# A decoder trunk in split fp32: more weight pairs by seven products, sums by DMAs that add, and an order with later loads

## The chip, the cores and the metric

One core of one Trainium2 chip runs the whole kernel. The metric is the device time of one execution in microseconds (us). The kernel before took 2121.14 us, the median of 3 runs (2120.87 to 2121.73).

## The reference

Two layers act on a residual stream x of 256 tokens by 2048 columns, all in float32. Each layer has a token mixer and an MLP, each behind an RMS norm and added to x. The mixers (forgetting attention in layer 0, dilated windows in layer 1) are not touched by the change. The MLPs are:

```
def sq_relu_mlp(h, w_up, w_down):
    a = jax.nn.relu(h @ w_up)
    return (a * a) @ w_down

for i in range(DEPTH):                      # 2 layers
    h = rms_norm(x, mix_norm_g[i])
    ...                                     # mixer
    x = x + mix
    h = rms_norm(x, mlp_norm_g[i])
    x = x + sq_relu_mlp(h, mlp_w_up[i], mlp_w_down[i])
```

h is 256 x 2048, w_up 2048 x 8192, w_down 8192 x 2048.

## The kernel before

**Split numbers.** Each fp32 operand is a high part (rounded to fp32r, a format that TensorE, PE, multiplies fast) and a low part, the rest. A product is three matmuls: high by high, low weight by high, high weight by low token (L386 to L388). `loaded` (L329) brings a pair of weight blocks (2 x 128 rows by 512 columns, 512 KB) into a raw buffer by a DMA on SP's queue; `cut` (L340) has ScalarE (ACT) cast the high part `hi` (L342) and VectorE (DVE) subtract it for the low part `lo` (L348). There are 6 raw, 4 hi and 4 lo buffers, and one more of each in the MLPs.

**Units.** A `Unit` (L352) makes 256 tokens by 512 columns from 8 such pairs. In the form `whole` (L376) a pair is 12 matmuls of 512 columns. In the form `parts` (L410) the pair's 2 x 2 blocks (two row blocks by two column halves, against two token tiles) are multiplied by seven products and not eight, a Strassen-Winograd scheme: DVE first makes three sums of weight blocks (L413 of 512 columns, L418 and L420 of 256) in a second raw buffer, two cuts follow (768 columns of the weights themselves, 1024 of sums), and PE runs 21 matmuls of 256 columns. The token sums (`sigma`) are made once per MLP. A unit that mixes both forms (`quarters`, L391, for its full pairs) needs the banks A and C and some additions at its end (L973 to L986). `HALVED` (L42) names the pairs of each up unit that go by seven products: 5 of 8 in the periods 1 to 3 of each MLP, none in period 0, so 120 pairs in the two MLPs.

**An MLP** (L1016) has 4 periods; each makes 4 up units (2048 of 8192 columns), and the 4 down units of the period before are merged in, a unit of each at a time, pair by pair in the order `UU_D`. The last period's down units stand alone at the end. At an up unit's end (`up_end`, L944) ACT brings the sums from PSUM, applies ReLU, DVE transposes blocks of 32 (L994), DMAs take the tile through DRAM and back (`through_dram`, L444), ACT squares (L1002), casts the high part of the tokens aT (L1007), and DVE makes the low part (L1009). At a down unit's end (`add_to_x`, L521) DVE adds both PSUM banks to x (L527).

**The order** is worked out while the program is built. `Plan` (L89) holds every operation with a cost in us (`on_act`, `on_dve`, `moved`, `WHOLE`, `QUARTER`); PE's products keep the order in which the code adds them, and every other operation gets a due time backwards from the product that needs it (`gap`: HANDOFF between engines, LANDING after a DMA). A forward pass (`run`) then takes, on each engine, the ready operation that is due first, and its times give each engine's fixed list. Engines run their lists in order and wait for each other by semaphores.

Of the kernel before, what the change touches and what calls it, by code (L numbers as in the profile page):

```python
# [13 lines left out]
ALU = mybir.AluOpType  # L14
# [3 lines left out]
P = 128  # L18
D = 2048
S = 256  # L20
NT = S // P
NC = 512
# [13 lines left out]
PERIODS = DFF // D  # L36
WHOLE = 6 * 0.2167
QUARTER = 0.112
ADDING = ()
FIVE = (0, 2, 4, 5, 7)  # L40
MORE = (1, 1, 1)
HALVED = [[(), (), (), ()], [FIVE] * 4, [FIVE] * 4, [FIVE] * 4]  # L42


def on_act(n, accum=False):
    return 0.24 + 0.00083 * n + (0.19 if accum else 0)


def on_dve(n, inputs=2):
    return 0.17 + (0.00104 if inputs == 2 else 0.00054) * n  # L50


def moved(kb):
    return kb / 380.0

# [33 lines left out]
class Plan:  # L89

    HANDOFF = 0.25
    LANDING = 2.1
    BACKLOG = 2.0
    FIRST = 14.0

# [39 lines left out]
    def gap(self, a, b):  # L137
        if a.eng == "dma":
            return self.LANDING
        if a.eng is None:  # L140
            return 0.0
        if a.eng == b.eng:
            return 0.0 if a.eng == "pe" else 0.06
        return self.HANDOFF

# [37 lines left out]
    def run(self):  # L183
# [18 lines left out]
        while events:  # L202
# [14 lines left out]
            if eng == "dma":  # L217
                landed = max(landed, now) + op.us
                free[eng] = max(now + 0.07, landed - self.BACKLOG)
# [9 lines left out]
def trunk(ctx: ExitStack, tc, x, fox_w_in, fox_b_f, fox_q_gain, fox_k_gain, fox_w_out, dil_w_in,  # L229
# [30 lines left out]
    N_HI = 4  # L260
    N_LO = 4
    N_Z = 1
    N_C = 1
# [7 lines left out]
    for ph in ("mlp0", "mlp1"):  # L271
        rings[ph] = dict(sigma=ring("sigma", 4, 2 * 4 * 2 * P, ph), tr=ring("tr", 4, NT * NC, ph),
                         z=ring("z", N_Z, 6 * S, ph), c=ring("c", N_C, NC, ph))
    for ph, n_sets, heads in (("fox", 1, 4), ("dil", 3, 2)):
# [169 lines left out]
    def through_dram(turned, into, size=NT * NC):  # L444
        blocks = blocks_ring.take()
        for i in range(4):
            def go(i=i):
                nc.sync.dma_start(v(blocks)[:, :, :, i, :].rearrange("t j c x -> c t j x"),
                                  v(turned)[32 * i:32 * i + 32, 0:size].rearrange("p (t j x) -> p t j x", t=NT, j=4))
            add("dma", 0.45, go, reads=[turned], writes=[(blocks, i)])  # L450

# [68 lines left out]

    def add_to_x(n, then=None):  # L521
        def end(banks):
            pair = banks[0].slot[0]

            def go():
# [417 lines left out]

    def up_end(l, phase, source, halved):  # L944
        own = rings[phase]

        def end(banks):
            z, turned = own["z"].take(), own["tr"].take()
            by = lambda t: v(f"rstd{l}")[:, t:t + 1]
# [50 lines left out]
            for t in range(NT):  # L1000
# [7 lines left out]
                writes=[(a, b, 0) for b in range(4)])  # L1008
            add("dve", on_dve(2 * NC), lambda: nc.vector.tensor_sub(r(a)[:, 2 * NC:], v(turned), v(a)[:, 0:2 * NC]),  # L1009
                reads=[*((turned, t) for t in range(NT)), *((a, b, 0) for b in range(4))], writes=[(a, b, 1) for b in range(4)])  # L1010
        return end

    AC, BE = ("A0", "A1", "C0", "C1"), ("B0", "B1")
    UU_D = "UUDUDUDUDUDUDUDD"

    def mlp(l, layer, phase, source, sigmas, then, last=None):  # L1016
# [6 lines left out]
        for b in range(PERIODS):  # L1023
            a = Source()
            ups = []
            for n in range(4):
                halved = HALVED[b][n]
                banks = AC if halved else ("A0", "A1") if b or n % 2 == 0 else ("B0", "B1")
                ups.append(Unit(source, mlp_w_up[layer], 0, [(b * D + n * NC, NC)], banks,
                                up_end(l, phase, a, halved), halved, sigmas))  # L1030
            if b == 0:
# [8 lines left out]
            for n in range(NX):  # L1040
                banks = ("E0", "E1") if turn % 2 == 0 else ("B0", "B1")
                turn += 1
                end = add_to_x(n, then if b == PERIODS - 1 else None)
                downs.append(Unit(a, mlp_w_down[layer], b * D, [(n * NC, NC)], banks, end, adding=ADDING if b < PERIODS - 1 else ()))
# [216 lines left out]
```

## Time and profile before

| | |
|---|---|
| runs, median (lowest to highest) | 2121.14 us (2120.87 to 2121.73) |
| profiled execution, its own time | 2121.22 us |
| its span, first to last instruction | 2119.5 us |
| PE busy | 2109.8 us (100%) |
| DVE busy | 1669.8 us (79%) |
| ACT busy | 1266.0 us (60%) |
| POOL busy | 57.8 us (3%) |
| DMA packets of SP's queue | 72.9% of 16 engines, 490.86 MB |
| granted PE clock | 1.00 |

PE is TensorE, PEld its weight loads, POOL is GpSimd, SP the engine that issues the DMAs. Busy shares are means over stages: in the merged periods of the MLPs (464 to 947 us in the first) DVE is busier than its mean. In a view of groups each row has line, engine, operation, out<-in, shape and count, then busy us, mean ns of one, and idle us before them with what ended it. In a list of waits a row has who waited for whom, us in total, times, longest.

### The profile page before, as it was taken

Reading aid. Unit: us, or ns where it says so; the run is one execution under the profiler, and the core shown is the slowest. Engines: PE = TensorE matmul, PEld = TensorE weight load, DVE = VectorE, ACT = ScalarE, POOL = GpSimd, SP = SyncE. Lnnn points to the kernel's source line nnn. Section 1 sums busy time; section 2 is a strip of 40 time slices with the busy share of each in tenths; the row PEclk is TensorE's granted clock in tenths of the full one; section 3 lists DMA queues with packets and bytes.
Section 4 is the critical chain, followed back from the end, with each engine's and each line's share of the span. In section 5 each row is a group of like instructions: output and inputs, shape, how many; then the busy total and the mean of one; then the engine's idle time right before and its main releaser. Section 6 shows DMA issues by size and latency. Waiting matters only on the chain.

```text
span 2119.5 us, 30432 instructions
## 1 busy us (share of the span) xinstructions
PE 2109.8 (100%) x11285; PEld 1888.0 (89%) x11285; DVE 1669.8 (79%) x2092; ACT 1266.0 (60%) x1640; POOL 57.8 (3%) x51
## 2 busy tenths in 40 slices
PE   9999999999999999999999999999999999999999
PEld 7888888889999999998888888888899999999988
DVE  6777777678899899886787777777678898898874
ACT  5555556566666666666555555556666666666652
POOL 1011000000000000000010000000000000000000
PEclk9999999999999999999999999999999999999999
DMA  7777668777767777777786776768767777777773
GB/s 247 233 221 199 212 217 262 240 243 238 228 225 242 241 225 237 245 257 260 227 259 200 235 223 207 249 203 285 237 223 232 249 228 230 248 229 228 248 259 129
DMA packets 336133, 492.93 MB, mean 233 GB/s; under 512 B 21928, under 2 KB 137712, under 8 KB 335984
## 3 DMA queue, kind: packets, MB, share of 16 engines
q1 hardware_dynamic: 335712, 490.86, 72.9%
q8 instruction: 88, 1.44, 0.3%
q14 instruction: 61, 0.50, 0.1%
q10 hardware_dynamic: 272, 0.13, 0.0%
HBM read 455.26 MB, written 35.65 MB: 232 GB/s over the span
## 4 chain that ended last, share of the span: by engine, by line
PE 99%; DMA 0%; SPq 0%; DVE 0%; issue 0%; ACT 0%
PE bank_B L386 11%; PE bank_B L388 11%; PE bank_B L387 11%; PE bank_C L407 9%; PE bank_A L386 7%; PE bank_A L388 7%; PE bank_A L387 7%; PE bank_E L386 7%; PE bank_E L388 7%; PE bank_E L387 7%; PE bank_A L437 3%; PE bank_A L438 3%; PE bank_A L436 3%; PE bank_C L437 2%; PE bank_C L438 2%; PE bank_C L436 2%
## 5 line engine op out<-in xcount | busy, mean ns | idle before, releaser
L342 ACT CAST hi<-raw 128x1024 fp32r<-128x1024 f32 (+1 forms) x720 | 736.0, 1026 | 585.0 <-PE bank_B L388 171.1
L348 DVE TENSOR_TENSOR lo<-raw,hi 128x1024 fp32r<-128x1024 f32 (+1 forms) x720 | 854.7, 1193 | 277.1 <-ACT hi L342 261.7
L386 PE MATMUL bank_A<-hi,hT 128*128 128x512 f32 x552 | 212.0, 384 | 0.0
L388 PE MATMUL bank_A<-hi,hT 128*128 128x512 f32 x552 | 210.3, 381 | 0.0
L387 PE MATMUL bank_A<-lo,hT 128*128 128x512 f32 x552 | 210.2, 381 | 0.0
L386 PE MATMUL bank_B<-hi,aT 128*128 128x512 f32 x520 | 197.5, 380 | 0.5 <-ACT aT L646 0.5
L388 PE MATMUL bank_B<-hi,aT 128*128 128x512 f32 x520 | 197.1, 379 | 0.0
L387 PE MATMUL bank_B<-lo,aT 128*128 128x512 f32 x520 | 197.1, 379 | 0.0
L386 PE MATMUL bank_B<-hi,hT 128*128 128x512 f32 x480 | 183.7, 383 | 0.0
L387 PE MATMUL bank_B<-lo,hT 128*128 128x512 f32 x480 | 181.9, 379 | 0.0
L388 PE MATMUL bank_B<-hi,hT 128*128 128x512 f32 x480 | 181.9, 379 | 0.0
L386 PE MATMUL bank_E<-hi,aT 128*128 128x512 f32 x472 | 179.0, 379 | 0.0
L387 PE MATMUL bank_E<-lo,aT 128*128 128x512 f32 x472 | 178.9, 379 | 0.0
L388 PE MATMUL bank_E<-hi,aT 128*128 128x512 f32 x472 | 178.9, 379 | 0.0
L342 ACT CAST mlp_hi<-raw 128x1024 fp32r<-128x1024 f32 (+1 forms) x108 | 109.7, 1016 | 90.1 <-PE bank_E L388 27.0
L348 DVE TENSOR_TENSOR mlp_lo<-raw,mlp_hi 128x1024 fp32r<-128x1024 f32 (+1 forms) x108 | 127.0, 1176 | 27.7 <-ACT mlp_hi L342 24.1
L407 PE MATMUL bank_C<-hi,hT 128*128 128x512 f32 x430 | 138.5, 379 | 0.0
L388 PEld LDWEIGHTS bank_A<-hi,hT 128*128 128x128 f32 x552 | 104.9, 190 | 15.4 <-DVE hT L711 0.5
L386 PEld LDWEIGHTS bank_A<-hi,hT 128*128 128x128 f32 x552 | 105.1, 190 | 14.0
L387 PEld LDWEIGHTS bank_A<-lo,hT 128*128 128x128 f32 x552 | 105.0, 190 | 14.1
L388 PEld LDWEIGHTS bank_B<-hi,aT 128*128 128x128 f32 x520 | 98.3, 189 | 14.1 <-DVE aT L647 0.2
L386 PEld LDWEIGHTS bank_B<-hi,aT 128*128 128x128 f32 x520 | 98.4, 189 | 13.3 <-ACT aT L646 0.7
(360 smaller groups left out, 4391.7 us busy)
## 6 DMA issues: line engine op xcount, KB each, us to landing
raw<-in_mlp_w_up_dram SPq DMA_DIRECT2D x222, 512.0 KB, 4.5
raw<-in_mlp_w_down_dram SPq DMA_DIRECT2D x222, 512.0 KB, 4.8
raw<-in_fox_w_in_dram SPq DMA_DIRECT2D x96, 512.0 KB, 4.6
raw<-in_dil_w_in_dram SPq DMA_DIRECT2D x192, 256.0 KB, 3.1
blocks<-mlp_tr SPq DMA_DIRECT2D x176, 128.0 KB, 3.6
mlp_z<-blocks SPq DMA_DIRECT2D x44, 512.0 KB, 5.4
mlp_raw<-in_mlp_w_up_dram SPq DMA_DIRECT2D x34, 512.0 KB, 4.5
mlp_raw<-in_mlp_w_down_dram SPq DMA_DIRECT2D x34, 512.0 KB, 4.6
```

What stands on the lines that cost most here:

```text
L342: add("act", on_act(n), lambda: nc.scalar.copy(r(hi)[:, 0:n], v(src)[:, at:at + n]), reads=keys, writes=[hi])
L348: add("dve", on_dve(n), lambda: nc.vector.tensor_sub(r(lo)[:, 0:n], v(src)[:, at:at + n], v(hi)[:, 0:n]), reads=[*keys, hi], writes=[lo])
L386: nc.tensor.matmul(acc, a, h, start=first and i == 0, stop=False)
L387: nc.tensor.matmul(acc, a, l, start=False, stop=False)
L388: nc.tensor.matmul(acc, b, h, start=False, stop=last and i == 1)
L407: nc.tensor.matmul(to, m, w, start=False, stop=False)
L436: nc.tensor.matmul(acc, a(0), w(0, at), start=first and edge & 1 == 1, stop=False)
L437: nc.tensor.matmul(acc, a(0), w(1, at), start=False, stop=False)
L438: nc.tensor.matmul(acc, a(1), w(0, at), start=False, stop=last and edge & 2 == 2)
```

## The change

- `HALVED` becomes a table with its own pairs for each up unit: 85 per MLP (6 in period 0, in one unit; 27, 26 and 26 in the periods 1 to 3) and so 170 in all.
- The residual additions of the down units of the periods 0 to 2 (12 per MLP) leave DVE: ACT copies the two PSUM banks to a buffer `sums` (L540 of the changed kernel), and a DMA issued by POOL adds the buffer to x (L530). The last period's additions stay on DVE.
- The low parts of aT of the first three up units of each period (12 per MLP): ACT writes the negative high part (L1032) and a DMA issued by POOL adds the token tile to it. The fourth unit's stays on DVE.
- The buffer `sums` takes the place of one of the four `tr` buffers, and serves as z in period 0's full units.
- The plan's numbers change: engines a little faster, LANDING 4.0 and not 2.1, 0.43 us on SP between two DMAs, loads at 335 and not 380 KB per us; `UU_D` is another merge of 8 up and 8 down pairs. All of this only sets the order. Matmuls go from 11210 to 11662, SP's DMAs stay at 1237, DVE's instructions between two tiles go from 1686 to 1848.

```diff
-WHOLE = 6 * 0.2167
+WHOLE = 6 * 0.2161
-HALVED = [[(), (), (), ()], [FIVE] * 4, [FIVE] * 4, [FIVE] * 4]
+HALVED = [[(), (), (0, 1, 3, 4, 5, 7), ()],
+          [(0, 2, 3, 5, 6, 7), (0, 1, 3, 4, 5, 6, 7), (0, 1, 3, 4, 5, 6, 7), (0, 1, 3, 4, 5, 6, 7)],
...
-    LANDING = 2.1
+    LANDING = 4.0
     BACKLOG = 2.0
+    ISSUE = 0.43
...
+    def added(to, of, reads, writes, us):
+
+        add("pool", 1.2, lambda: nc.gpsimd.dma_start(to(), of(), accum_op=ALU.add), reads=[*reads, *writes])
+        add("dma", us, None, reads=reads, writes=writes)
...
+            if room is not None:
+                sums = room.take()
+                for t in range(NT):
+                    def go(t=t):
+                        nc.scalar.copy(halves(v(sums)[:, t * NC:(t + 1) * NC], S), by_column(v(banks[t]), S))
+                    add("act", on_act(NC), go, reads=[banks[t]], writes=[(sums, t)])
+                added(lambda: v(f"x{n}"), lambda: v(sums), [(sums, t) for t in range(NT)], x_keys(n), 2.55)
+                return
...
-            add("dve", on_dve(2 * NC), lambda: nc.vector.tensor_sub(r(a)[:, 2 * NC:], v(turned), v(a)[:, 0:2 * NC]),
-                reads=[*((turned, t) for t in range(NT)), *((a, b, 0) for b in range(4))], writes=[(a, b, 1) for b in range(4)])
+            if by_dma:
+                add("act", on_act(2 * NC), lambda: nc.scalar.mul(r(a)[:, 2 * NC:], v(turned), -1.0), reads=whole, writes=low)
+                added(lambda: v(a)[:, 2 * NC:], lambda: v(turned), whole, low, 2.55)
+            else:
+                add("dve", on_dve(2 * NC), lambda: nc.vector.tensor_sub(r(a)[:, 2 * NC:], v(turned), v(a)[:, 0:2 * NC]),
+                    reads=[*whole, *((a, b, 0) for b in range(4))], writes=low)
...
-    UU_D = "UUDUDUDUDUDUDUDD"
+    UU_D = "UUUDUDUDDUUDUDDD"
```

What this does to the engines' lists, at three places. First DVE near the start of the first merged period of MLP 0, where a halved pair's raw buffer is loaded again. In before, the buffer mlp0_raw0 has its last reader in the first row, and the pair loaded into it next is needed in the last:

```order
L348 TENSOR_TENSOR lo1_131<-mlp0_raw0_2629,hi1_127 128x1024
L418 TENSOR_TENSOR raw4_124<-raw4_124,raw3_123 128x256
L420 TENSOR_TENSOR raw4_124<-raw4_124,raw3_123 128x256
L348 TENSOR_TENSOR lo2_132<-raw2_122,hi2_128 128x1024
L348 TENSOR_TENSOR lo3_133<-raw3_123,hi3_129 128x768
L413 TENSOR_TENSOR raw2_122<-mlp0_raw0_2629 128x512
```

In the changed kernel at the same place, with buffer raw4 (L355, L420, L425 and L427 are the old L348, L413, L418 and L420):

```order
L355 TENSOR_TENSOR mlp0_lo0_2616<-raw4_124,mlp0_hi0_2615 128x1024
L355 TENSOR_TENSOR lo0_130<-raw5_125,hi0_126 128x1024
L355 TENSOR_TENSOR lo1_131<-raw0_120,hi1_127 128x1024
L355 TENSOR_TENSOR lo2_132<-raw1_121,hi2_128 128x1024
L355 TENSOR_TENSOR lo3_133<-mlp0_raw0_2614,hi3_129 128x1024
L420 TENSOR_TENSOR raw3_123<-raw2_122 128x512
L355 TENSOR_TENSOR mlp0_lo0_2616<-raw2_122,mlp0_hi0_2615 128x768
L425 TENSOR_TENSOR raw3_123<-raw3_123,raw2_122 128x256
L420 TENSOR_TENSOR raw5_125<-raw4_124 128x512
```

Four rows stand between the last reader and the new need in before, seven now.

Second POOL in MLP 0. In before nothing stands between the two reciprocal roots of the norms around the MLP:

```order
L552 TENSOR_TENSOR sm8_88<-sm7_87,mhalf_65 128x8
L472 TENSOR_TENSOR rstd1_75<-sm17_97,mhalf_65 128x2
L472 TENSOR_TENSOR rstd2_77<-sm18_98,mhalf_65 128x2
L742 IOTA dil_s0_8211 128x128
L743 IOTA dil_s0_8211 128x256
```

Now 24 DMAs that add stand there, of which these are the first:

```order
L479 TENSOR_TENSOR rstd1_75<-sm17_97,mhalf_65 128x2
L530 DMA aT0_116<-mlp0_tr1_2609 128x1024
L530 DMA aT1_117<-mlp0_tr2_2610 128x1024
L530 DMA aT2_118<-mlp0_tr0_2608 128x1024
L530 DMA x0_68<-mlp0_sums0_2613 128x1024
L530 DMA x1_69<-mlp0_sums0_2613 128x1024
L530 DMA x2_70<-mlp0_sums0_2613 128x1024
L530 DMA aT0_116<-mlp0_tr2_2610 128x1024
```

POOL's list in the MLPs goes from empty to one DMA per 20 us or so, and nothing else is queued there.

Third DVE towards the end of a merged period of MLP 0. In before the low parts of two token tiles (L1009) stand among the weights' rows:

```order
L420 TENSOR_TENSOR raw0_120<-raw0_120,raw5_125 128x256
L1009 TENSOR_TENSOR aT1_117<-mlp0_tr1_2624,aT1_117 128x1024
L413 TENSOR_TENSOR raw3_123<-raw2_122 128x512
L348 TENSOR_TENSOR lo0_130<-raw5_125,hi0_126 128x768
L348 TENSOR_TENSOR lo1_131<-raw0_120,hi1_127 128x1024
L418 TENSOR_TENSOR raw3_123<-raw3_123,raw2_122 128x256
L1009 TENSOR_TENSOR aT2_118<-mlp0_tr2_2625,aT2_118 128x1024
L420 TENSOR_TENSOR raw3_123<-raw3_123,raw2_122 128x256
L973 TENSOR_TENSOR mlp0_z0_2627<-mlp0_z0_2627,mlp0_c0_2628 128x2x256
L974 TENSOR_TENSOR mlp0_z0_2627<-mlp0_z0_2627 128x256
L975 TENSOR_TENSOR mlp0_z0_2627<-mlp0_z0_2627 128x256
L348 TENSOR_TENSOR lo2_132<-raw1_121,hi2_128 128x1024
```

In the changed kernel there, from the low part lo2 to the low part lo0, which a matmul of a later halved pair needs:

```order
L355 TENSOR_TENSOR lo2_132<-mlp0_raw0_2614,hi2_128 128x1024
L355 TENSOR_TENSOR lo3_133<-raw2_122,hi3_129 128x1024
L420 TENSOR_TENSOR raw4_124<-raw3_123 128x512
L355 TENSOR_TENSOR mlp0_lo0_2616<-raw3_123,mlp0_hi0_2615 128x768
L425 TENSOR_TENSOR raw4_124<-raw4_124,raw3_123 128x256
L1005 TENSOR_TENSOR mlp0_z0_2611<-mlp0_z0_2611,mlp0_c0_2612 128x2x256
L1006 TENSOR_TENSOR mlp0_z0_2611<-mlp0_z0_2611 128x2x256
L427 TENSOR_TENSOR raw4_124<-raw4_124,raw3_123 128x256
L355 TENSOR_TENSOR lo1_131<-raw5_125,hi1_127 128x1024
L355 TENSOR_TENSOR lo0_130<-raw4_124,hi0_126 128x1024
```

The token tiles' rows are gone from this place, and the three sums of the next halved pair stand closer together among the low parts.

More of the change, by code (lines that the diff above doesn't have):

```diff
@@ L142, in gap @@
         if a.eng == b.eng:
-            return 0.0 if a.eng == "pe" else 0.06
-        return self.HANDOFF
+            return 0.0 if a.eng == "pe" else 0.12
+        return 0.3 if a.eng == "pe" else self.HANDOFF
     def order(self, rounds=3):
@@ L261, in trunk @@
     N_LO = 4
+    N_TR = 3
     N_Z = 1
@@ L449, in go @@
                                   v(turned)[32 * i:32 * i + 32, 0:size].rearrange("p (t j x) -> p t j x", t=NT, j=4))
-            add("dma", 0.45, go, reads=[turned], writes=[(blocks, i)])
+            add("dma", 0.5, go, reads=[turned], writes=[(blocks, i)])
         def back():
@@ L941, in trunk, with up_end @@
     out_proj(oT, fox_w_out[0], then1)
-    def up_end(l, phase, source, halved):
+    def up_end(l, phase, source, halved, by_dma, room):
         own = rings[phase]
         def end(banks):
-            z, turned = own["z"].take(), own["tr"].take()
+            z, turned = own[room].take(), own["tr"].take()
             by = lambda t: v(f"rstd{l}")[:, t:t + 1]
@@ L1042, in mlp @@
                 turn += 1
-                end = add_to_x(n, then if b == PERIODS - 1 else None)
+                end = add_to_x(n, then) if b == PERIODS - 1 else add_to_x(n, None, rings[phase]["sums"] if BY_DMA else None)
                 downs.append(Unit(a, mlp_w_down[layer], b * D, [(n * NC, NC)], banks, end, adding=ADDING if b < PERIODS - 1 else ()))
```

26 lines of the change are left out of this document (15 added, 11 removed), and 2 rows, old and new, of the table HALVED.

## The prediction

> **What bounds the kernel now.** I read the page's totals first, then the chain that ended last, then who TensorE (PE) waited for. The profiled execution took 2121.22 us, its span 2119.5 us, so 1.7 us lie around the span; the median of the three runs shown is 2121.14 us, 0.08 lower. My sums start from 2121.22.
>
> ```profile
> span 2119.5 us, 30432 instructions
> PE 2109.8 (100%) x11285; PEld 1888.0 (89%) x11285; DVE 1669.8 (79%) x2092; ACT 1266.0 (60%) x1640; POOL 57.8 (3%) x51
> PE 99%; DMA 0%; SPq 0%; DVE 0%; issue 0%; ACT 0%
> ```
>
> PE is 99% of the chain. A busy PE may still hide stalls, so I asked for its waits; this is the whole list:
>
> ```profile
> PE bank_E L701 <- DMA x<-in_x_dram: 2.1, 2, 1.7
> PE bank_C L659 <- POOL ident masks.py:199: 1.7, 1, 1.7
> PE bank_E L670 <- DMA fox_s<-in_mix_norm_g_dram: 1.3, 1, 1.3
> PE bank_B L1191 <- DVE x L1206: 0.8, 1, 0.8
> PE bank_B L386 <- ACT aT L646: 0.5, 1, 0.5
> ```
>
> Three belong to the first 9 us, one to the last 10, one to an attention head. In both MLPs PE never waits: the time is the sum of matmuls, and what shortens that sum shortens the kernel until something else comes late. So I need two numbers: what PE saves, and how much room VectorE (DVE), which makes every low part, has left. Here are the three merged periods of the first MLP (us, then busy time and count of PE, PEld, DVE, ACT and POOL, clock, DMA share, GB/s):
>
> ```profile
> 464.00:625.00 161.00, 161.00 (x954) 146.94 (x953) 140.81 (x173) 102.53 (x120) 0.00 (x0) 1.00 0.73 234
> 625.00:786.00 161.00, 161.00 (x954) 146.94 (x953) 143.57 (x177) 103.03 (x120) 0.00 (x0) 1.00 0.74 236
> 786.00:947.00 161.00, 161.00 (x943) 146.63 (x942) 142.02 (x171) 102.49 (x119) 0.00 (x0) 1.00 0.76 246
> ```
>
> DVE is busy 426.4 of 483 us (88%), ACT 308.1 (64%), POOL not at all; the granted clock is 1.00.
>
> **The change part by part.**
>
> *Fifty more pairs by seven products.* The chain of one unit of before (8 up pairs, 5 of them halved, and 8 down pairs):
>
> ```profile
> 463.85 1.73 PE bank_C L407 x8
> ...
> 473.10 2.59 PE bank_C L407 x12
> ...
> 488.15 2.59 PE bank_C L407 x12
> ...
> 504.07 1.73 PE bank_C L407 x8
> ```
>
> A pair in full is 12 matmuls of 512 columns, 2.59 us. The unit repeats after 504.07 - 463.85 = 40.22 us; its 11 full pairs take 28.5, so a halved pair takes (40.22 - 28.5) / 5 = 2.34 us. Each of the 50 pairs saves 0.25 us: **12.5 us**. The two units that are now halved in the first periods start their banks with one 512-column matmul cut in two, under 0.02 us.
>
> *What that costs DVE.* The timeline of DVE within that unit (start, length, idle before):
>
> ```profile
> 469.28 1.23 DVE L348 TENSOR_TENSOR mlp_lo<-raw,mlp_hi 128x1024 fp32r<-128x1024 f32 x1 [0.92 <-ACT mlp_hi L342]
> 470.42 0.95 DVE L348 TENSOR_TENSOR lo<-raw,hi 128x768 fp32r<-128x768 f32 x1
> 471.29 0.69 DVE L413 TENSOR_TENSOR raw<-raw 128x512 f32<-128x512 f32 x1
> 471.89 1.22 DVE L348 TENSOR_TENSOR lo<-mlp_raw,hi 128x1024 fp32r<-128x1024 f32 x1
> 473.03 0.42 DVE L418 TENSOR_TENSOR raw<-raw,raw 128x256 f32<-128x256 f32 x1
> 473.49 0.43 DVE L420 TENSOR_TENSOR raw<-raw,raw 128x256 f32<-128x256 f32 x1
> 474.26 1.23 DVE L348 TENSOR_TENSOR lo<-raw,hi 128x1024 fp32r<-128x1024 f32 x1 [0.35 <-ACT hi L342]
> 476.64 0.96 DVE L348 TENSOR_TENSOR lo<-raw,hi 128x768 fp32r<-128x768 f32 x1 [1.15 <-ACT hi L342]
> 479.77 0.69 DVE L413 TENSOR_TENSOR raw<-mlp_raw 128x512 f32<-128x512 f32 x1 [2.17 <-DMA mlp_raw<-in_mlp_w_up_dram]
> 480.50 0.42 DVE L418 TENSOR_TENSOR raw<-raw,mlp_raw 128x256 f32<-128x256 f32 x1
> 480.84 1.22 DVE L348 TENSOR_TENSOR mlp_lo<-raw,mlp_hi 128x1024 fp32r<-128x1024 f32 x1
> ```
>
> Neighbours overlap, so a row costs the distance of the starts: 1.14 us for 1024 columns (471.89 to 473.03), 0.87 for 768, 0.60 for 512, 0.34 for 256. A halved pair adds a low part of 768 and three sums: 0.87 + 0.60 + 2 x 0.34 = 2.15 us. An MLP's merged periods get 27 + 26 + 26 = 79 halved pairs in place of 60: 19 x 2.15 = 40.9 us. The other 6 pairs per MLP lie in the first period, where DVE has room to spare.
>
> *What the DMAs that add take off DVE.* In the merged periods 12 residual additions and 9 low parts per MLP leave it, each a 1024-column row (three more low parts leave the first period):
>
> ```profile
> L527 DVE TENSOR_TENSOR x<-x,bank_B 128x1024 f32<-128x1024 f32 x6 | 7.3, 1213 | 0.3 <-PE bank_B L388 0.3
> L1009 DVE TENSOR_TENSOR aT<-mlp_tr,aT 128x1024 fp32r<-128x1024 f32 x12 | 14.6, 1218 | 1.3 <-ACT aT L1007 1.2
> L968 ACT COPY mlp_z<-bank_A 128x512 f32<-128x512 f32 x12 | 7.1, 590 | 0.0
> L1007 ACT CAST aT<-mlp_tr 128x1024 fp32r<-128x1024 f32 x12 | 12.7, 1058 | 7.9 <-PE bank_B L387 7.8
> L342 ACT CAST hi<-raw 128x768 fp32r<-128x768 f32 x37 | 30.9, 836 | 34.6 <-PE bank_E L388 13.6 <-PE bank_C L407 7.7 <-PE bank_B L388 7.6
> ```
>
> 21 x 1.14 = 23.9 us. So DVE goes to 426.4 + 40.9 - 23.9 = 443.4 us while PE's time falls to 483 - 19 x 0.25 = 478.2: 93%, with **34.8 us of room left** of 56.6. ACT gets 12 x 2 copies of 0.59, 9 passes that make the negative high part, 1.06 each like the cast, and 19 casts of 0.84: 308 + 40 = 348 of 478, 73%; both stay below PE, so I cost these edits at nothing while that holds. Behind a copy that waits for its bank stand casts that PE needs, but copies of that kind stand so in before too (the L968 row), with no PE wait.
>
> *Does the room lie where it is needed?* A low part can start once PE has freed its buffer and ACT has cast (1.06 us, about 1.4 with both handovers, an estimate), and all DVE rows from there to the next low part that PE needs must fit before it. I summed this over every such stretch in the order of both kernels, with the costs above. The tightest of before has 1.16 us to spare, and PE lost nothing there. The tightest of the changed order has 1.16 us too. The stretch shown last in the section on the change: 54 matmuls of 0.112 us (2.34 / 21) and 23 of 0.216 (2.59 / 12) give 11.0 us, less 1.4 for the cast; DVE's ten rows are 7.9, and 1.5 is left after the handover. But there are now 18 low parts with under 1.6 us to spare, where before had 4. Nothing stalls by count; less forgives lateness.
>
> *The adding DMAs themselves.* Before has none; the nearest rows:
>
> ```profile
> q1 hardware_dynamic: 69141, 114.43, 73.8%
> raw<-in_mlp_w_up_dram SPq DMA_DIRECT2D x79, 512.0 KB, 4.3
> mlp_z<-blocks SPq DMA_DIRECT2D x12, 512.0 KB, 5.8
> ```
>
> In these 482 us 114.43 MB took 73.8% of the engines, so 512 KB takes 1.63 us of all sixteen. An add that reads two streams may take twice that; as ends, 1.63 to 3.3 us of the engines, and 4.3 to 5.8 us, or 9 if twice as much to move counts, until it lands. I take 5.8, the slower of the two rows. Who waits for it: the third matmul of the next down unit reads the low part. By the order's matmuls it comes at least 10.7 us after the DMA is issued, mostly 14 to 30; x is read a unit later. The end of 9 us is covered too: **nothing**, up to 10.7 us.
>
> *The order that counts loads later.* DVE waits 2.17 us above for a load; its issue:
>
> ```profile
> 473.14 0.37 SPq L335 DMA_DIRECT2D mlp_raw<-in_mlp_w_up_dram  x1
> ```
>
> It took 6.6 us, and DVE had four rows (2.7 us) to do between the buffer's last reader and the new need. Of the up loads that DVE reads first, 28 of 120 in before have under 4 us of DVE work as cover; in the changed order 2 of 144, with a median of 6.8. Loads and DVE waits in the merged periods:
>
> ```profile
> DVE raw L413 <- DMA raw<-in_mlp_w_up_dram: 15.9, 16, 1.8
> DVE lo L348 <- ACT hi L342: 25.0, 40, 1.1
> ACT hi L342 <- PE bank_E L388: 35.0, 27, 1.8
> ```
>
> Most of those 15.9 us go, which gives DVE back half of the room that it loses; the 25.0 behind ACT, which waits for PE, shrink by themselves when DVE gets busier. PE waited for none of these, so the term is 0. Start and end of the program keep their first and last rows.
>
> **The sum.** 2121.2 - 12.5 + 0 = **2108.7 us** (against the median of before, 0.6% faster).
>
> **Rivals.**
>
> *Loads come late behind the adds.* The adds share the engines with the weights, now 74% taken: 21 x 1.63 to 3.3 us in 478 makes 82 to 89%. A load beside an add lands 1.63 us later. For it speaks that 18 low parts have under 1.6 us to spare; against it, the cover of 6.8 us over a landing of 4.3. If all 18 (both MLPs together) met such a load, each would cost 1.63 - 1.16 = 0.47: 8.5 us; half of them, 4.2: **2113 us**. At the end of 3.3 us, 18 x 2.1 = 38.5 us. The Trainium skill's page "DMA: Bandwidth & Descriptors", section "Queues, rings and completion order", says that each engine takes turns between queues packet by packet; by that rule an add beside a load halves the load's rate while both run, which is this rival. No run here shows it yet: before moves its data on one queue, q1.
>
> *DVE itself loses time to each add, and becomes the bound.* With t us lost per add, DVE's 34.8 us of room are gone at t = 34.8 / 21 = 1.66; beyond that PE waits 42 x (t - 1.66). The gain is eaten at t = 1.96. The nearest row of a POOL instruction:
>
> ```profile
> L552 POOL TENSOR_TENSOR sm<-sm,mhalf 128x8 f32<-128x8 f32 x20 | 42.2, 2109 | 459.2 <-DVE sm L550 459.2
> ```
>
> If an issue on POOL took these 2.11 us and DVE stood still meanwhile: 42 x 0.45 = 18.9, so 2108.7 + 18.9 = **2127.6 us**, slower than before; twice that time would cost 107 us. For it: POOL was idle in these stages, so nothing shows the two side by side. Against: it needs DVE to stand for nearly the whole issue. The skill's page "SBUF — State Buffer", section "Who interferes with whom", says that DVE and GpSimd lock one shared port pair, but that a DVE instruction with two SBUF inputs locks out only GpSimd's reads, and infers that writing descriptors is not among these. By that rule t is about 0 and the forecast stands; no run here shows it.
>
> **How the numbers follow.** Forecast, no new wait beyond 3 us (2107 to 2112): 0.62. Late loads: 0.24, of which 0.18 end below 2116.9 and 0.06 between that and 2125.4. DVE-bound: 0.14. What a measurement of this kernel can tell from no change is about 0.2%, 4.2 us. So faster 0.62 + 0.18 = 0.80, same 0.06, slower 0.14. The low end is the forecast with the waits of 0.5 and 0.8 us gone too, and 0.4 us for rounding in 50 x 0.25: 2107.0. The high end takes in the late loads of 8.5 us and a little more, 2118.5; above lie the slower case and a part of the late loads, together under 0.2.
>
> **What would show it.** Right: merged units of 39.7 us (seven halved: 7 x 2.34 + 9 x 2.59) and PE with no waits in the MLPs; DVE busy near 93% there; the row L413's waits for loads well below 15.9 us; matmuls that never wait for an aT from a DMA. Late loads: PE waits of 0.2 to 1 us behind a DVE low part whose own predecessor waited for raw. DVE-bound: DVE rows longer than 1.22 us or gaps while a POOL DMA is issued, units beyond 40.2 us, and PE waiting for lo in every unit. I am wrong altogether if the halved pairs pace PE at more than 2.34 us, or if a first matmul on a DMA-made aT waits, which means adds that land after more than 10.7 us.

## The result, and the profile after

| | before | changed |
|---|---|---|
| runs, median (lowest to highest), us | 2121.01 (2120.55 to 2121.73) | 2109.39 (2108.96 to 2110.39) |
| ratio of the times, with its 95% interval | | 0.9946 (0.9928 to 0.9963) |
| profiled execution, its span, us | 2121.22, 2119.5 | 2109.11, 2107.4 |

The changed kernel is 0.5% faster: 11.6 us by the medians, 12.1 us by the profiled spans; the forecast was 2108.7. The totals from the page of the changed kernel:

```profile
span 2107.4 us, 31766 instructions
PE 2096.8 (99%) x11737; PEld 1891.4 (90%) x11737; DVE 1723.3 (82%) x2254; ACT 1342.7 (64%) x1770; POOL 100.4 (5%) x99
```

PE is still what the kernel's time is made of. The changed kernel's whole list of PE's waits (us in total, times, longest):

```profile
PE bank_E L721 <- DVE hT L731: 2.2, 1, 2.2
PE bank_E L690 <- DMA fox_s<-in_mix_norm_g_dram: 1.8, 1, 1.8
PE bank_C L679 <- POOL ident masks.py:199: 1.7, 1, 1.7
PE bank_B L1217 <- DVE x L1232: 0.8, 1, 0.8
PE bank_C L663 <- DVE fox_pl L652: 0.3, 1, 0.3
```

None of them lies in an MLP. The first three belong to the program's start and come to 5.7 us, against 5.1 before. The three merged periods of the first MLP together in the changed kernel (us, busy time and count of PE, PEld, DVE, ACT and POOL, clock, DMA share, GB/s):

```profile
464.00:943.00 479.00, 479.00 (x3022) 442.52 (x3021) 442.69 (x575) 341.45 (x416) 18.96 (x22) 1.00 0.85 264
```

PE has no idle time there; DVE is at 442.7 of 479 us (92%), ACT at 71%. The chain of the changed kernel, one unit with seven of its eight up pairs halved:

```profile
504.86 1.73 PE bank_C L414 x8
...
544.59 1.73 PE bank_C L414 x8
```

The unit repeats after 39.73 us, where five halved pairs took 40.22. DMA queues and issues of the changed kernel in 464 to 943 us (a queue's row has packets, MB and the share of 16 engines; q0 is that of POOL's adds. The last number of an issue's row is the median from issue to landing):

```profile
q1 hardware_dynamic: 69135, 114.41, 72.1%
q0 software_dynamic: 3140, 11.42, 12.5%
...
raw<-in_mlp_w_up_dram SPq DMA_DIRECT2D x79, 512.0 KB, 5.1
...
x<-mlp_sums POOLq DMA_DIRECT2D x12, 512.0 KB, 7.5
...
aT<-mlp_tr POOLq DMA_DIRECT2D x10, 512.0 KB, 8.3
```

The 22 adds took 12.5% of 479 us, 59.9 us, or 2.7 us of all sixteen engines each. They land in 7.5 and 8.3 us (medians), and a load now takes 5.1 us and not 4.3. That median hides two kinds of loads: one issued at 506.61 us, beside the add shown below, and one issued at 498.60, before it:

```profile
raw<-in_mlp_w_up_dram SPq DMA_DIRECT2D x1, 512.0 KB, 7.5
...
raw<-in_mlp_w_up_dram SPq DMA_DIRECT2D x1, 512.0 KB, 4.6
```

All that DVE waited there for up loads, from the changed kernel's list of waits:

```profile
DVE raw L420 <- DMA raw<-in_mlp_w_up_dram: 0.5, 1, 0.5
```

The 15.9 us in which DVE waited for raw buffers are down to 0.5, although a load is 0.8 us slower in the median. Last, POOL's timeline at one add, and DVE's at the same time:

```profile
504.55 0.86 POOL L530 DMA_DIRECT2D x<-mlp_sums  x1 [31.13 <-ACT mlp_sums L540]
```

```profile
504.17 0.95 DVE L355 TENSOR_TENSOR lo<-raw,hi 128x768 fp32r<-128x768 f32 x1
505.03 0.41 DVE L427 TENSOR_TENSOR raw<-raw,raw 128x256 f32<-128x256 f32 x1
505.37 1.21 DVE L355 TENSOR_TENSOR lo<-raw,hi 128x1024 fp32r<-128x1024 f32 x1
```

POOL issues from 504.55 to 505.41; DVE's three rows that touch this stretch last 0.95, 0.41 and 1.21 us, as everywhere else.

### The profile page after: what moved, and what is told of

The parts are those of the page before. It is cut to its first block, busy times and chain, and to the rows that moved or that the text cites. A ratio compares the mean times of both kernels' runs of the same rounds, so it can differ in the third digit from the quotient of the medians.

```text
span 2107.4 us, 31766 instructions
## 1 busy us (share of the span) xinstructions
PE 2096.8 (99%) x11737; PEld 1891.4 (90%) x11737; DVE 1723.3 (82%) x2254; ACT 1342.7 (64%) x1770; POOL 100.4 (5%) x99
## 4 chain that ended last, share of the span: by engine, by line
PE 99%; DMA 0%; DVE 0%; ACT 0%; issue 0%; SPq 0%
PE bank_B L393 11%; PE bank_B L395 11%; PE bank_B L394 11%; PE bank_E L393 7%; PE bank_E L395 7%; PE bank_E L394 7%; PE bank_A L393 6%; PE bank_A L394 6%; PE bank_A L395 6%; PE bank_C L414 4%; PE bank_A L445 4%; PE bank_A L444 4%; PE bank_A L443 4%; PE bank_C L444 3%; PE bank_C L445 3%; PE bank_C L443 3%
## 5 line engine op out<-in xcount | busy, mean ns | idle before, releaser
L355 DVE TENSOR_TENSOR lo<-raw,hi 128x1024 fp32r<-128x1024 f32 (+1 forms) x754 | 880.0, 1178 | 263.3 <-ACT hi L349 249.2
L349 ACT CAST hi<-raw 128x1024 fp32r<-128x1024 f32 (+1 forms) x754 | 756.0, 1014 | 515.5 <-PE bank_B L395 151.2
L393 PE MATMUL bank_B<-hi,aT 128*128 128x512 f32 x552 | 209.4, 379 | 0.0
L395 PE MATMUL bank_B<-hi,aT 128*128 128x512 f32 x552 | 209.2, 379 | 0.0
L393 PE MATMUL bank_A<-hi,hT 128*128 128x512 f32 x496 | 190.7, 384 | 0.0
L394 PE MATMUL bank_A<-lo,hT 128*128 128x512 f32 x496 | 188.6, 380 | 0.0
L395 PE MATMUL bank_A<-hi,hT 128*128 128x512 f32 x496 | 188.5, 380 | 0.0
L393 PE MATMUL bank_E<-hi,aT 128*128 128x512 f32 x440 | 166.9, 379 | 0.0
L395 PE MATMUL bank_E<-hi,aT 128*128 128x512 f32 x440 | 166.8, 379 | 0.0
L355 DVE TENSOR_TENSOR mlp_lo<-raw,mlp_hi 128x1024 fp32r<-128x1024 f32 (+1 forms) x118 | 137.0, 1161 | 20.7 <-ACT mlp_hi L349 19.7
L395 PEld LDWEIGHTS bank_B<-hi,aT 128*128 128x128 f32 x552 | 104.3, 189 | 14.8
L394 PEld LDWEIGHTS bank_B<-lo,aT 128*128 128x128 f32 x552 | 104.5, 189 | 13.6
L393 PEld LDWEIGHTS bank_B<-hi,aT 128*128 128x128 f32 x552 | 104.5, 189 | 13.6
L443 PE MATMUL bank_A<-hi,mlp_sigma 128*128 128x256 f32 x396 | 108.9, 275 | 0.0
L444 PE MATMUL bank_A<-lo,mlp_sigma 128*128 128x256 f32 x396 | 108.9, 275 | 0.0
L445 PE MATMUL bank_A<-hi,mlp_sigma 128*128 128x256 f32 x396 | 108.9, 275 | 0.0
```

The source lines that it names most:

```text
L349: add("act", on_act(n), lambda: nc.scalar.copy(r(hi)[:, 0:n], v(src)[:, at:at + n]), reads=keys, writes=[hi])
L355: add("dve", on_dve(n), lambda: nc.vector.tensor_sub(r(lo)[:, 0:n], v(src)[:, at:at + n], v(hi)[:, 0:n]), reads=[*keys, hi], writes=[lo])
L393: nc.tensor.matmul(acc, a, h, start=first and i == 0, stop=False)
L394: nc.tensor.matmul(acc, a, l, start=False, stop=False)
L395: nc.tensor.matmul(acc, b, h, start=False, stop=last and i == 1)
L443: nc.tensor.matmul(acc, a(0), w(0, at), start=first and edge & 1 == 1, stop=False)
```

## The experiments

The change has four parts that can be taken apart: the 50 more pairs, the two kinds of adds, and the plan's numbers. The new merge `UU_D` and the new set of buffers stay in every run, so what they alone are worth at 170 pairs is not shown. All times are medians; each ratio is against the kernel before on the same chip (2120.73, 2120.79 and 2121.13 us in the three groups of runs, so times of different groups compare within 0.4 us), with its 95% interval.

### The pairs alone, the order alone

**120 pairs, all the rest as changed.**

```diff
-HALVED = [[(), (), (0, 1, 3, 4, 5, 7), ()],
...
+HALVED = [[(), (), (), ()], [FIVE] * 4, [FIVE] * 4, [FIVE] * 4]
```

> The changed kernel with the 120 pairs of before: the adding DMAs and the planning numbers stay. Theory (time is the sum of PE's matmuls, the pairs alone carry the gain): 2121 us, 2120 to 2122, and no PE waits in the MLPs, with DVE at about 82% in the merged periods (426 - 24 of 483). Rival (the adds or the order bring some of the 11.6 us by themselves): under 2119 us.

Measured 2122.0 us, ratio 1.0008 (0.9999 to 1.0017). Without the pairs nothing is gained: adds and order bring no time of their own. DVE is busy 409.9 of 483 us (85%, not 82). It also waits 17.4 us for up loads in the first MLP's merged periods (464 to 947 us), with the same adds and plan numbers with which the changed kernel's DVE waited 0.5; the largest row:

```profile
DVE raw L417 <- DMA raw<-in_mlp_w_up_dram: 12.5, 10, 3.7
```

PE waits for none of it. So neither the adds nor the plan's numbers fix by themselves how long DVE waits for loads, and with 120 pairs such waits cost nothing.

**120 pairs, no adds, the changed plan.**

```diff
-BY_DMA = True
-LOW_BY_DMA = True
+BY_DMA = False
+LOW_BY_DMA = False
...
+HALVED = [[(), (), (), ()], [FIVE] * 4, [FIVE] * 4, [FIVE] * 4]
```

> The kernel before's 120 pairs and no adding DMAs, with the changed kernel's plan numbers and merge of the pairs: the order alone. Theory (PE never waited in the MLPs before, so an order has nothing to give back): 2119 to 2122.5, DVE's waits for loads far below 15.9 us per MLP. Rival (the order is a gain of its own): below 2116.

Measured 2121.35 us, ratio 1.0002 (0.9993 to 1.0010). DVE's waits for raw in its first MLP's merged periods (464 to 947 us):

```profile
DVE raw L417 <- DMA raw<-in_mlp_w_up_dram: 0.5, 1, 0.5
```

They fell from 15.9 to 0.5 us and the time stayed: with 120 pairs PE waits for none of this, and shorter waits that PE never felt give nothing back.

### The adds

**170 pairs, no adds.**

```diff
-BY_DMA = True
-LOW_BY_DMA = True
+BY_DMA = False
+LOW_BY_DMA = False
```

> The 170 pairs and the new planning numbers, with all residual additions and low parts back on DVE; no adding DMA. Theory (DVE's room decides): DVE needs 442.7 + 23.9 = 466.6 of 479 us in the merged periods, 97%; by the count of its rows 4 low parts of the whole kernel are short of time by up to 0.2 us and 44 have under 1.6 us to spare, so PE waits a little: 2110 to 2114 us. Rival 1 (the adds are what makes the gain possible): 2118 us or more. Rival 2 (DVE has room either way, the adds buy nothing): 2109.4 us.

Measured 2115.68 us, ratio 0.9976 (0.9967 to 0.9985): between the theory's range and the first rival's. Nearly the whole loss hangs on two places, one in each MLP. PE's wait there, then ACT's timeline around the first, and the transposes on DVE that belong to it, in this run and in the changed kernel:

```profile
PE bank_A L443 <- ACT mlp_z L988: 3.3, 2, 1.7
```

```profile
691.18 0.59 ACT L988 COPY mlp_c<-bank_A 128x512 f32<-128x512 f32 x1 [0.17 <-PE bank_A L445]
...
697.49 1.14 ACT L1022 ACTIVATE mlp_tr<-mlp_z 128x512 f32<-128x512 f32 x2
699.34 1.04 ACT L349 CAST hi<-raw 128x1024 fp32r<-128x1024 f32 x1 [0.70 <-PE bank_B L395]
700.29 0.58 ACT L988 COPY mlp_z<-bank_A 128x512 f32<-128x512 f32 x1
```

```profile
682.73 1.24 DVE L1014 STREAM_TRANSPOSE mlp_tr<-mlp_z 128x1024 f32<-128x1024 f32 x1
```

```profile
669.03 1.23 DVE L1014 STREAM_TRANSPOSE mlp_tr<-mlp_z 128x1024 f32<-128x1024 f32 x1
```

An up unit ends at about 691: ACT copies the first part of bank A at once, but the rest of the bank 9 us later. It goes into the one z buffer, which the unit before holds until its squares (L1022) have read it, from 697.49 to 698.63. Those squares come after the transposes, which stand 13.7 us later in the fuller DVE list, and after the way through DRAM, whose last DMA is issued at 690.44 and lands 6.7 us later. PE issues its last matmul before bank A at 698.9 and then waits. The squares are not the last step: by 698.63 the z buffer is free, but in ACT's fixed list a cast stands before the copy, and that cast itself waits for PE until 699.34. In the second MLP the rows are the same (squares until 1783.50, the cast at 1784.21, the copy at 1785.16). So the late z buffer and the place of the copy in ACT's list make the wait together. That is a chain that no low part shows.

**170 pairs, only the residual additions by DMA.**

```diff
-LOW_BY_DMA = True
+LOW_BY_DMA = False
```

> 170 pairs and the changed kernel's plan; the 24 residual additions by adding DMAs, the 24 low parts back on DVE. With both on DVE the time was 2115.7 us, and the trace had one unit end per MLP where PE waited for a bank that ACT copied out late (1.83 us), the second time followed by 256-column matmuls at half pace. By the order's count of DVE's room the tightest stretch is -0.18 us with all on DVE, 0.66 with the sums by DMA, 1.16 with both. Theory (the adds are worth just those late copies, and half of the room is enough): 2109 to 2112, no such wait. Rival (each addition is worth its share of the 6.3 us): 2112 to 2114.

Measured 2108.85 us, ratio 0.9944 (0.9932 to 0.9957): the theory, 0.15 us under its range, and PE waits nowhere in the MLPs. Its windows row for the merged periods:

```profile
464.00:943.00 479.00, 479.00 (x3022) 442.54 (x3021) 452.23 (x585) 333.28 (x406) 10.55 (x12) 1.00 0.81 254
```

PE has no idle time with DVE at 452.2 of 479 us (94%). The 24 low parts by DMA bring nothing that can be measured: this kernel's ratio and the changed one's, 0.9944 and 0.9946, lie well inside each other's interval.

**170 pairs, only the low parts by DMA.**

```diff
-BY_DMA = True
+BY_DMA = False
```

> The other half: the 24 low parts by adding DMAs, the 24 residual additions on DVE; 170 pairs, the changed kernel's plan. The tightest stretch by the order is 0.66 us here too. Theory (half of the room is enough): 2109 to 2112 and no wait for a copied bank. Rival (each addition is worth its share): 2112 to 2114.

Measured 2114.33 us, ratio 0.9970 (0.9958 to 0.9981): the theory that half of the room is enough, whichever half, falls, and the time lies 0.3 us above the rival's range. PE's largest wait in its MLPs, and its windows row:

```profile
PE bank_A L444 <- DVE lo L355: 2.4, 4, 0.9
```

```profile
464.00:943.00 479.00, 477.17 (x3009) 440.23 (x3008) 450.47 (x582) 329.25 (x389) 8.62 (x10) 1.00 0.80 250
```

The late copies of the bank are gone here too, but low parts come late instead (also those of the tokens aT that DVE makes, 1.2 us), with no more DVE work than in the run before. The tightest stretch by my count is 0.66 us in both orders, so the count does not tell them apart. What differs is where the rows lie in the two lists; which of them is to blame I did not isolate.

### The plan's numbers

**All of the plan's old numbers.** Pairs, adds and the merge of the pairs stay as changed.

```diff
-WHOLE = 6 * 0.2161
+WHOLE = 6 * 0.2167
...
-    return kb / 335.0
+    return kb / 380.0
-    HANDOFF = 0.2
-    LANDING = 4.0
+    HANDOFF = 0.25
+    LANDING = 2.1
-    ISSUE = 0.43
+    ISSUE = 0.07
...
```

(on_act's constant goes from 0.12 back to 0.24, on_dve's from 0.085 to 0.17, and the gaps between engines and one DMA's cost, 0.5 to 0.45, as well.)

> The changed kernel in an order worked out with the numbers of before (engine costs, LANDING 2.1, handovers, 0.07 us between DMAs); pairs, adds and UU_D as changed. Theory (the order that counts loads later is needed): by the count of DVE rows 6 low parts are short of time by up to 3.1 us and loads have less cover, so DVE waits for loads again (10 us or more per MLP) and PE for DVE: 2113 to 2120 us. Rival (the numbers only shift who waits off the path): 2109.4 us, within 1.

Measured 2178.07 us, ratio 1.0270 (1.0256 to 1.0284): the direction was right, the size was missed by 58 us and more. The next three runs take the numbers apart, all but that one DMA's cost.

**Only LANDING.**

```diff
-    LANDING = 4.0
+    LANDING = 2.1
```

> The changed kernel with one number of its plan set back: a load counts as landed 2.1 us after its issue and not 4.0; pairs, adds and all other numbers as changed. The run with all of the plan's old numbers took 2178.1 us, 69 more than the changed kernel. Theory 1 (the late loads did that: DVE waited 34.8 us for raw there, 0.5 us in the changed kernel, while a load lands in 5.1 us): most of the 69 us come back, 2140 to 2180, with DVE waits for raw of 20 us and more per MLP. Theory 2 (ACT's place for the copies of the banks did it, which the engines' costs set): 2109 to 2115, with PE waits under 3 us in all in the MLPs although DVE waits for some loads.

Measured 2172.29 us, ratio 1.0242 (1.0225 to 1.0259): theory 1. Its DVE list around one place of the second MLP, then PE's largest wait of the run and PE's clock there (windows of PE alone: us, busy time, clock, DMA share, GB/s):

```profile
1798.25 0.42 DVE L427 TENSOR_TENSOR mlp_raw<-mlp_raw,raw 128x256 f32<-128x256 f32 x1
...
1803.77 0.69 DVE L420 TENSOR_TENSOR raw<-raw 128x512 f32<-128x512 f32 x1 [3.21 <-DMA raw<-in_mlp_w_up_dram]
...
1805.51 1.22 DVE L355 TENSOR_TENSOR lo<-mlp_raw,hi 128x1024 fp32r<-128x1024 f32 x1
```

```profile
PE bank_A L444 <- DVE lo L355: 23.8, 17, 4.3
```

```profile
1805.00:1810.00 5.00, 3.21 (x13) 0.53 0.63 183
1810.00:1815.00 5.00, 5.00 (x19) 0.78 0.89 316
1815.00:1820.00 5.00, 5.00 (x42) 1.00 0.69 238
```

DVE stands 3.21 us at the head of its list for a raw buffer. The low part of mlp_raw, whose sums were done at 1798.67 and which needs nothing from that buffer, stands behind it and ends at 1806.73; PE waited for it until 1806.8, 4.3 us by the list. By my count of DVE rows, which no view shows, this order has the same room as the changed kernel (tightest 1.16 us), so the room is not what it lacks: its loads stand too late for a landing of 5.3 us in the median. The load of this place was issued at 1795.43, 1.7 us after an add (1793.69), and took 8.2 us. After the wait PE goes on at 0.53 and 0.78 of its clock.

**Only the engines' costs, handovers and a pair's length.**

```diff
-WHOLE = 6 * 0.2161
+WHOLE = 6 * 0.2167
...
-    return 0.12 + 0.00083 * n + (0.19 if accum else 0)
+    return 0.24 + 0.00083 * n + (0.19 if accum else 0)
...
-    HANDOFF = 0.2
+    HANDOFF = 0.25
...
```

> The other half: the plan's costs of ACT and DVE, the handovers and the length of a pair as before, but loads counted as in the changed kernel (4.0 us until landed, 0.43 between issues, 335 KB per us). Theory 1 (loads): the time stays near the changed kernel's, 2109 to 2120, with DVE's waits for raw under 5 us per MLP. Theory 2 (ACT's place for the copies and casts): 2140 to 2180, with PE waiting for the banks that ACT copies out, 10 us and more in all. If both this run and the one with 2.1 us lie near 2109, neither number alone is needed, only one of the two.

Measured 2144.8 us, ratio 1.0113 (1.0100 to 1.0127): theory 2 by the time, and so both groups of numbers are needed. PE waited 9.4 us for copied banks, a little under the 10 of the theory, and 9.6 us more for the tokens aT that ACT (6.5) and DVE (3.1) made late. ACT's timeline in this run, and in the changed kernel at the same unit end:

```profile
530.23 0.58 ACT L988 COPY mlp_c<-bank_A 128x512 f32<-128x512 f32 x1
...
541.63 1.15 ACT L1022 ACTIVATE mlp_tr<-mlp_z 128x512 f32<-128x512 f32 x2 [1.23 <-DMA mlp_z<-blocks]
542.68 0.56 ACT L988 COPY mlp_z<-bank_A 128x512 f32<-128x512 f32 x1
```

```profile
526.37 1.15 ACT L1022 ACTIVATE mlp_tr<-mlp_z 128x512 f32<-128x512 f32 x2
...
530.96 0.59 ACT L988 COPY mlp_c<-bank_A 128x512 f32<-128x512 f32 x1 [0.17 <-PE bank_A L445]
531.45 0.59 ACT L988 COPY mlp_z<-bank_A 128x512 f32<-128x512 f32 x1
```

In the changed kernel the unit before has been squared when the bank is full, so the copies follow at once. With the old costs the squares come 15 us later, the bank is free at 543.2, and PE waited for it from 537.9: 5.17 us by the starts of its matmuls. It is the chain of the run with no adds, drawn out: the transposes of that unit start at 529.48 on DVE, where the changed kernel has them at 509.78, and the tile's way through DRAM ends only when the squares begin.

**Only SP's numbers.**

```diff
-    return kb / 335.0
+    return kb / 380.0
...
-    ISSUE = 0.43
+    ISSUE = 0.07
```

> The changed kernel with the third group of plan numbers set back: 0.07 us between SP's issues and not 0.43, loads at 380 and not 335 KB per us; LANDING stays 4.0 and the engines' costs as changed. LANDING alone set back cost 63 us, the engines' costs alone 35, all three 69. Theory (what counts is how long before its need a load is due, and here this falls little: median cover 6.1 us against 6.8): 2109 to 2114, DVE waits for raw under 8 us per MLP. Rival (any old number breaks the order): 2125 and more.

Measured 2112.64 us, ratio 0.9962 (0.9950 to 0.9975). The time is as the theory has it; DVE's waits for up loads came to 17.2 us (13.6 + 2.4 + 1.2) and not to under 8; the largest row:

```profile
DVE raw L420 <- DMA raw<-in_mlp_w_up_dram: 13.6, 11, 2.5
```

PE waited 2.0 us for low parts, and 1.8 us more than in the changed kernel for hT of the first mixer, which is outside the MLPs. So in this run DVE lost 17 us to loads in one MLP nearly free of charge, with no single wait over 2.5 us, while the run with LANDING 2.1 lost 36.9 us there in waits of up to 4.0. The three groups' losses, 63, 35 and 3 us, do not add up to the 69 of all together: that they hit the same stretches is likely, but not shown.

### How much further

**202 pairs.**

```diff
+HALVED = [[(), (), (0, 1, 3, 4, 5, 7), ()], [tuple(range(8))] * 4, [tuple(range(8))] * 4, [tuple(range(8))] * 4]
```

> All eight pairs of every up unit in the periods 1 to 3 by seven products, 202 in all; the rest as changed. PE's sum alone falls by 32 x 0.25 = 8 us, to 2101.4. Theory (DVE becomes the bound where its work passes PE's): per MLP DVE needs 442.7 + 17 x 2.15 = 479.3 us where PE needs 474.8, so at least 2 x 4.5 us come back, and by the count 66 low parts are short by up to 3.7 us: 2110 to 2125 us, with DVE at 98% or more and PE waiting for lo in most units. Rival (room on DVE is no limit yet): 2101 to 2104 us.

Measured 2168.94 us, ratio 1.0225 (1.0211 to 1.0239), 44 us above the theory's range, where the matmuls alone would give 2109.4 - 32 x 0.25 = 2101.4. The two largest of PE's waits:

```profile
PE bank_A L441 <- DVE lo L352: 13.8, 16, 1.4
PE bank_A L440 <- ACT mlp_z L985: 13.7, 4, 3.4
```

Low parts and copied banks come late in about equal parts; I had counted only the first. Nor is DVE's sum the bound that the theory took: it is busy 451.0 of 479 us (94%), not 98%. What PE waits for is when single results come, and the sum of DVE's work does not tell that.

**180 pairs.**

```diff
+SEVEN = (0, 1, 3, 4, 5, 6, 7)
+HALVED = [[(), (), (0, 1, 3, 4, 5, 7), ()], [SEVEN] * 4, [SEVEN] * 4, [SEVEN] * 4]
```

> The changed kernel with 7 of 8 pairs halved in every up unit of the periods 1 to 3: 180 pairs. The matmuls alone would give 2109.4 - 10 x 0.25 = 2106.9 us. DVE's room by the order: two stretches short, by up to 0.9 us, 42 under 1.6 us (changed kernel: none short, 18). Theory (a count with short stretches means late banks, as with all additions on DVE, where 4 were short by 0.18 and the time lay 6.3 us over its matmuls): 2109 to 2118, slower than the changed kernel, with PE waits in the MLPs. Rival (only the two short stretches count): 2107 to 2109, the fastest kernel.

Measured 2113.37 us, ratio 0.9963 (0.9950 to 0.9977). The time is as the theory has it; PE's largest wait in the MLPs:

```profile
PE bank_A L442 <- DVE lo L353: 3.7, 2, 1.9
```

Two waits of up to 1.9 us, one in each MLP, fit the count's two short stretches; that they are the same places no view shows. They alone, 3.7 us, cost more than the 2.5 that ten pairs save. So 170 pairs lie near the edge for this order of things: beside it on the same chip the run with the sums alone took 2108.59 to 2109.87 us, this one 2112.4 to 2114.97.

**The fourth low part by DMA as well.**

```diff
-up_end(l, phase, a, halved, LOW_BY_DMA and n < 3, "z" if b or halved else "sums"), halved, sigmas))
+up_end(l, phase, a, halved, LOW_BY_DMA, "z" if b or halved else "sums"), halved, sigmas))
```

> The changed kernel with the fourth up unit's low part made by an adding DMA too: 32 low parts and not 24. These 8 have 5.4 to 7.7 us by the order's matmuls from the DMA's issue to the first matmul that reads the result; the 24 others have 11.2 us and more. An add landed 6.3 to 9.3 us after its issue, 8.0 in the middle, in the changed kernel. Theory (landing counts, and it is 8 us here): PE waits for aT behind a DMA in up to 8 places, 0.3 to 2.6 us each, 5 to 15 us in all, 2113 to 2125. Rival (an add lands in 5.8 us when few others run, as the prediction took): no more than two such waits, 2109 to 2112.

Measured 2117.4 us, ratio 0.9983 (0.9974 to 0.9992). The two largest of PE's waits in its MLPs:

```profile
PE bank_E L395 <- DMA aT<-mlp_tr: 3.4, 2, 2.2
...
PE bank_C L414 <- DVE lo L355: 1.7, 2, 1.1
```

Two of the eight adds were late. They were issued at 649.04 and 1734.70 us and PE went on at 654.8 and 1741.9, so even these had landed within 5.7 and 7.2 us, below the changed kernel's median; the other six met their matmuls in time. By the trace seven of the eight landed 4.9 to 5.9 us after their issue, near the 5.8 of the prediction, and one after 7.1. The other large waits are for low parts, in an order that has moved. The time lies with the theory, the landing and the number of waits with the rival: only 3.4 us of the 8 lost are waits for an add.

**The best version** is the one with the residual additions alone by DMA, 2108.85 us. It cannot be told from the changed kernel by time, and needs 24 fewer DMAs.

## Why the prediction was right

**PE and the pairs.** The step of 50 x 0.25 = 12.5 us was right: the unit of seven halved pairs measures 39.73 us (39.7 was named), and the spans differ by 12.1. Two small errors lie in this agreement, and they cancel. The wait list grew from 6.4 us in all to 6.8 (0.6 more at the start of the program, which I had taken as unchanged, 0.2 less in the attention heads), and from the start of the last matmul to the end of the span it now takes 4.0 us, not 3.6. Against these 0.8 us the matmuls saved a little more than the sum says: PE's busy time fell by 13.0 us (2109.8 to 2096.8). That the forecast came within 0.7 us of the median is in part luck. The run with 120 pairs shows that the pairs are the whole gain.

**DVE's load.** 443.4 us were worked out, 442.7 measured; the distances of the starts, 1.14 us for 1024 columns and so on, were the right price, not the rows' durations.

**The room by the count.** For the changed kernel it was right: none short, no wait. As a rule it is only half of one. It counts DVE rows between a buffer's release and the low part, and leaves out (1) the loads, so the order with LANDING 2.1 has the same tightest stretch by my count and loses 63 us, and (2) the way from a full bank to its copy, over the transposes, DRAM, squares and the single z buffer, which is what breaks first with no adds. I passed over (2) with the remark that copies stand behind casts in before as well; it was the nearest danger, and what keeps it off is either kind of add (with the low parts alone by DMA the late copies are gone too) and the plan's costs. The prediction weighed neither against this chain, so that it held here was luck.

**The adds.** Their landing was mis-sized: 5.8 us taken, 7.5 and 8.3 measured in the median, 9.5 at most, a little over the end of 9. It changed nothing because the cover of 10.7 us lay beyond it. 2.7 us of the engines lies between the 1.63 and 3.3 that I kept, and the DMA share of 0.85 between 82 and 89%. That the adds pay at all was argued from the sum of DVE's room; the runs show that the residual additions pay 6 to 7 us (2115.68 to 2108.85), and for the low parts nothing clear of the noise (2108.85 to 2109.39 with the residual additions, 2115.68 to 2114.33 without).

**The order.** The term 0 against before is what the run with the order alone gives. But the sentence that PE waited for none of these, so that the term is 0, holds at 120 pairs only. At 170 the same numbers decide between 2109 and 2178 us. I had the cover in hand (28 of 120 loads with under 4 us before) and did not ask what it would cost with the room nearly gone.

**Late loads behind the adds.** The rival's time fell, but its first step was right. A load beside an add did land later, and by more than the 1.63 us taken: 7.3 against 4.9 us in the median, as the last section has it. What failed is the next step, that the tight low parts would meet such a load: DVE waited 0.5 us in the merged periods of the first MLP, and PE not at all. It is not that loads cannot hurt, as the run with LANDING 2.1 shows, and with 120 pairs the same adds left DVE 17.4 us of waits. This order had room for them, and the prediction had only the median cover of 6.8 us to say so, less than what such a load takes.

**DVE standing still for each add.** This fell as well: DVE's rows of 1024 columns last 1.219 us on the mean against 1.220 before, and an issue takes 0.86 us and not 2.11. The Trainium skill's page "SBUF — State Buffer", section "Who interferes with whom", had inferred that writing descriptors is not locked out by a DVE instruction with two SBUF inputs; the rows shown above (0.95, 0.41 and 1.21 us beside an issue) agree.

## What to carry to other kernels

Ask of a change that fills an idle engine not only whether its busy share stays below the bound's, but which chains of handovers run through it, and follow each of them to the bound: weights, and also banks, single buffers and round trips. A planner's numbers may be off without harm while there is room, and cost many times the gain when it is nearly gone, so measure landings and durations under the load that the change itself makes. And test the parts of a bundle one by one: half of the adds here were worth nothing that could be measured.

## What the runs showed of the hardware

**A wait of PE costs more than its length.** In four runs I split PE's loss against the changed kernel by the distances of the starts of neighbouring matmuls: gaps over 0.25 us, and matmuls at up to twice their pace.

| run | span, us more than changed | gaps, us | slower matmuls, us |
|---|---|---|---|
| old plan | 70.1 | 53.5 | 16.7 |
| LANDING 2.1 | 68.7 | 51.7 | 17.1 |
| old engine costs | 35.0 | 26.2 | 8.4 |
| 202 pairs (8 us less to do) | 54.3 | 47.2 | 15.7 |

The second part is the granted clock. With the old engine costs, after the wait of 5.17 us from 537.9, matmuls of 256 columns start every 213 ns until 548.5 and every 111 ns from then on; the windows of PE in that run:

```profile
545.00:550.00 5.00, 5.00 (x32) 0.65 0.50 146
550.00:555.00 5.00, 5.00 (x29) 1.00 0.77 231
```

All 14 waits of 3 us and more in these four runs were followed by such matmuls, 1.1 to 2.5 us lost within 16 us. Shorter waits were mixed: with LANDING 2.1 the clock stood at 0.66 in the 5 us after a single wait of 2.35 us at 628.3, and stayed at 1.00 after one of 1.99 at 684.8; of the two of 1.83 us in the run with no adds the one at 698.9 left the clock at 1.00, and after the one at 1783.7 it stood at 0.68 in 1785 to 1790. The Trainium skill's page "TensorE: Matmul & The Clock Gate", section "Part 1: The HAM clock gate", puts the fall to half clock after an idle window of about 3.4 us that runs freely. Twelve of the 14 long waits are as long as that and agree; the other two (3.09 and 3.30 us) and the ones of 2.35 and 1.83 us are shorter than the page's window and were followed by slow matmuls all the same, and there the measurement decides.

**A DMA that adds** 512 KB within SBUF takes 2.7 us of the sixteen engines, 1.7 times a load's 1.63, and 0.86 us of POOL to issue.

**A load beside such an add lands later.** I sorted the 512 KB loads of weights in the merged periods of both MLPs whose landing the trace has (464 to 943 and 1560 to 2030 us) by whether an add was under way, from the end of its issue to its landing, for at least 2 of the load's first 4.3 us. These are medians from issue to landing:

| run | beside an add, us (loads) | others, us (loads) |
|---|---|---|
| changed | 7.3 (63) | 4.9 (136) |
| residual additions alone by DMA | 7.0 (31) | 5.0 (168) |
| low parts alone by DMA | 6.7 (31) | 4.8 (166) |
| 120 pairs | 6.4 (41) | 5.2 (140) |

The DMAs of the way through DRAM slow loads as well. Without any of those beside them, the changed kernel's loads land in 7.3 us beside an add (40 loads) and in 4.5 us else (73).
